# Output projections of two feed-forward blocks: nine pairs of weight tiles by seven products instead of eight, and no plain tile between the two passes

## The chip, the cores and the metric

One core of one Trainium2 chip. The metric is the device time of one execution in microseconds, as the median of several runs. TensorE is called PE in the profile, its weight loads PEld, VectorE DVE, ScalarE ACT, GpSimd POOL, and SyncE, which only issues transfers here, SP.

## The reference

One encoder layer on 512 tokens of width 1024 in float32: a feed-forward block (FFN), a mixer, and a second FFN.

```
def swiglu(x, w_in, w_out):
    gate, up = jnp.split(x @ w_in, 2, axis=-1)
    return (jax.nn.silu(gate) * up) @ w_out        # 1024 -> 2 x 2816 -> 1024

h = swiglu(rmsnorm(x, norm_ffn1_pre[l]), w_ffn1_in[l], w_ffn1_out[l])
x = x + FFN_RESIDUAL_SCALE * rmsnorm(h, norm_ffn1_post[l])
h = mixer(rmsnorm(x, norm_mix_pre[l]), ...)        # gated convolution, two-way mLSTM, output projection
x = x + rmsnorm(h, norm_mix_post[l])
h = swiglu(rmsnorm(x, norm_ffn2_pre[l]), w_ffn2_in[l], w_ffn2_out[l])
x = x + FFN_RESIDUAL_SCALE * rmsnorm(h, norm_ffn2_post[l])
```

The change lies in the output projection of each FFN, `(...) @ w_out`, a sum over 2816 hidden channels, and in three small places around.

## The kernel before

**Precision.** Every operand of a matmul is split into a high part (a rounding copy on ACT, `whi`) and a low part (the rest, a subtraction on DVE, `wlo`), by `split` (L352, L355) or `split_free` (L359, L360). A product is three matmuls: high by high, high by low, low by high. `split` is pinned: its DVE operation keeps its place in program order. `split_free` is not.

**Hidden channels.** 2816 channels are 22 tiles of 128, called k. For each k, `ffn` forms gate and up from 8 k tiles of the input and writes `h[k]`, 128 x 512 (channels by tokens). From the third k on, gate and up together take seven products in place of eight block products (Strassen's scheme in Winograd's form; L498, 20 passes of a loop with the variable `j`).

**Output projection.** The result is four blocks of 128 tokens by two halves of 512 columns: eight banks of PSUM, `acc[tb][half]`. A plain k tile gives 4 x 2 x 3 matmuls of 512 columns (`mm_out`, L673). A pair of k tiles, with the tokens cut in an early and a later half, is a 2 x 2 by 2 x 2 block product and is done by seven products of 2 x 3 matmuls each (`product_out`, L651). The seven sums do not fit in the banks together, so there are two passes over the pairs:

- pass a: products 1, 6, 7, 5 of every pair. Its left factors are sums of quarters of `h` (`left_a`, two pairs at a time, made in place in `h`), its right factors sums of quarters of `w_out` (`w_out_a`). An `a` item of weights is two half tiles and an own quarter (SP) and a quarter added by an accumulating transfer (POOL, L168).
- after the last pair of pass a, `taken` moves the banks into SBUF: a copy on ACT (L661) and six DVE operations (L605), pinned.
- pass b: products 2, 3, 4 of every pair, with `left_b` and `w_out_b`. A `b` item is one tile (SP, L200) and a quarter that POOL adds onto a kept sum (L188).

`SPLIT = (8, 5)` says: eight pairs (16 of 22 tiles) by seven products, and five plain tiles at the end (the tail), token block by token block, each block followed by its norm (`post_norm`). The one tile that is left is done plainly between the passes, and the first `left_b` is formed there.

**Order.** `w_get(n)` hands out the next weights and splits n items ahead. Raw weights go through four buffers (`rawp`), split ones through twelve (`wpool`), and the large tiles `h`, factors, sums through thirteen (`big`). The order on each engine is laid out beforehand by a planner which takes the instruction of the earliest place in the program that is ready by its own reckoning, except where instructions are pinned, or put behind another one by `tc.issue_after`. TensorE's matmuls are not pinned in the output projections.

**Residual.** `x_t` are four tiles of 128 x 1024 in `xpool`, which has just four. In the first FFN they hold x from the start to the end; after it they go to DRAM (`x_d`, L825) and are loaded again late in the mixer (L1322), for the second FFN.

**Mixer.** Behind four projections of one tile each (`plain_o`) comes `weigh_q` (L1101, L1107): four matmuls that spread decay factors, and eight DVE operations that weight the queries by them. `combine_x` forms the sums and splits of the mixer's input for its seven-product groups.

Of the kernel before, what the change touches and what calls it, by code (L numbers as in the profile page):

```python
# [28 lines left out]
SPLIT = ((8, 5), (8, 5))  # L29
# [3 lines left out]
PLAIN = 2  # L33
BW = 528
# [4 lines left out]
def encoder_kernel(ctx: ExitStack, tc: tile.TileContext, a: dict, out: bass.AP):  # L39
# [322 lines left out]
    def rstd(parts, n, mul, tag="rs"):  # L362
        w = parts[0].shape[1]
        acc = None
        for p_ in parts:
            t = sm([P, 4], tag=tag)
            if acc is None:
                pin(nc.vector.tensor_scalar(
                    out=t[:, 0:w], in0=p_, scalar1=mul / n, scalar2=mul * EPS, op0=ALU.mult, op1=ALU.add))
            else:  # L370
                pin(nc.vector.scalar_tensor_tensor(
                    out=t[:, 0:w], in0=p_, scalar=mul / n, in1=acc, op0=ALU.mult, op1=ALU.add))
# [94 lines left out]
    def post_norm(tb, acc, g, mul, after=None, order=(0, 1)):  # L467
        t = [t2() for _ in range(2)]

        def weigh(i):  # L470
            nc.vector.tensor_tensor(out=t[i], in0=acc[i], in1=g[:, blk(i, 512)], op=ALU.mult)

        s0 = sumsq(acc[order[0]])
        weigh(order[0])
        r = rstd([s0, sumsq(acc[order[1]])], D, mul)
        weigh(order[1])
        for i in range(2):
            h = blk(i, 512)
            nc.vector.scalar_tensor_tensor(out=x_t[tb][:, h], in0=t[i], scalar=r, in1=x_t[tb][:, h], op0=ALU.mult, op1=ALU.add)
            if after:  # L480
                after(tb, h)
# [20 lines left out]
    def ffn(xq, between, finish, mid=None, within=None, ahead=(2, 2, 1, 1), late=None, prep=None, block=0):  # L502
# [89 lines left out]
        later, early = slice(256, 512), slice(0, 256)  # L592
# [7 lines left out]

        def hcol(k):
            return h[k // 4][:, k % 4, 0:512]

        def tt(o, a_, b_, op, order=lambda v: None):
            order(nc.vector.tensor_tensor(out=o, in0=a_, in1=b_, op=op))  # L605

        def halves(g):
            if g == 1:
                t = bigt(F32R).rearrange("p q f -> p (q f)")
                return t[:, 0:1024].rearrange("p (g f) -> p g f", g=1), t[:, 1024:2048].rearrange("p (g f) -> p g f", g=1)  # L610
            return tuple(
                bigt(F32R).rearrange("p q f -> p (q f)")[:, 0:2048].rearrange("p (g f) -> p g f", g=2) for _ in range(2))

        def parts(hi, lo, g, at):
            return [{n: (hi[:, i, c:c + 256], lo[:, i, c:c + 256]) for n, c in at.items()} for i in range(g)]

        def group(i):
            g = min(2, seven - i)
            v = h[i // 2].rearrange("p (g e) f -> p g e f", e=2)[:, 0:g, :, 0:512]
            return g, v[:, :, 0], v[:, :, 1]  # L620

        def left_a(i):
            g, a_, b_ = group(i)
            hi, lo = halves(g)
            s1 = t4()[:, 0:256 * g].rearrange("p (g f) -> p g f", g=g)
            tt(s1, a_[:, :, early], b_[:, :, early], ALU.subtract)
            split_free(hi[:, :, 0:256], lo[:, :, 0:256], a_[:, :, later])
            tt(a_[:, :, early], a_[:, :, later], a_[:, :, early], ALU.subtract)
            tt(a_[:, :, later], a_[:, :, early], b_[:, :, early], ALU.add)
            split_free(hi[:, :, 256:512], lo[:, :, 256:512], s1)  # L630
            split_free(hi[:, :, 512:1024], lo[:, :, 512:1024], a_)
            return parts(hi, lo, g, {1: 0, 5: 256, 7: 512, 6: 768})

        def left_b(i):
            g, a_, b_ = group(i)
            hi, lo = halves(g)
            split_free(hi[:, :, 0:512], lo[:, :, 0:512], b_)
            tt(a_[:, :, early], b_[:, :, later], a_[:, :, later], ALU.subtract)
            split_free(hi[:, :, 512:768], lo[:, :, 512:768], a_[:, :, early])
            return parts(hi, lo, g, {4: 0, 2: 256, 3: 512})  # L640
# [48 lines left out]
        hs, plain_n = None, 0  # L689
        ks = {}  # L690
        for at, (kind, n) in enumerate(order):
# [13 lines left out]
            elif kind == "a":  # L705
                if n % 2 == 0 and n:
                    lefts = left_a(n)
                left, right = lefts[n % 2], w_get(1)
                for m in ((1, 6, 7, 5) if n else (6, 7, 5)):
                    product_out(m, left, right, n == 0, n == seven - 1)  # L710
                    if n == seven - 1:
                        taken(m)
            else:
                if n % 2 == 0:
# [3 lines left out]
                for m in (2, 3, 4):  # L718
                    product_out(m, left, right, False, False)

# [449 lines left out]
    weigh_k()  # L1170
    plain_o(3)
    weigh_q()
# [154 lines left out]
    for tb in range(NT):  # L1327
# [12 lines left out]
        xs[tb] = pre_norm(tb, g_pre3)  # L1340

# [36 lines left out]
```

## Time and profile before

| | |
|---|---|
| median of 3 runs | 894.24 us (893.87 to 894.26) |
| the profiled execution | 893.36 us, of which the span is 891.6 us |
| PE, DVE, ACT, POOL busy | 883.4, 716.3, 485.5, 86.6 us |
| granted TensorE clock | 0.999 |
| read from HBM, written | 109.66 MB, 4.19 MB |

The span runs from the first to the last instruction of the program on the core. Busy shares are averages over stages with different limits, so the stages are looked at one by one. A row such as `DVE L355 TENSOR_TENSOR wlo<-raw,whi 128x1024 ... x1` names engine, line, operation, what is written from what, the shape and the count; in front stand start and length in microseconds, behind, in brackets, how long the engine was idle before and what ended that.

### The profile page before, as it was taken

The numbers are of one execution on the slowest core, as the hardware profiler recorded it, in microseconds if no ns is written. First come the engines' busy times: TensorE is split into PE (matmuls) and PEld (weight loads), VectorE is DVE, ScalarE is ACT, GpSimd is POOL, SyncE is SP. The second block draws the span as 40 slices with busy tenths as digits, with TensorE's granted clock in tenths as the row PEclk, the third lists the DMA queues.
The fourth block names the chain that finished last, engine by engine and source line by source line (L and its number), as shares of the span: only waits on it lengthen the run. The fifth ranks groups of instructions, "written<-read, shape, count | busy, mean of one in ns | idle before, by whom it ended". The sixth has DMA issues, their size and how long they took to land.

```text
span 891.6 us, 15212 instructions
## 1 busy us (share of the span) xinstructions
PE 883.4 (99%) x6007; PEld 810.1 (91%) x6007; DVE 716.3 (80%) x1109; ACT 485.5 (54%) x824; POOL 86.6 (10%) x108
## 2 busy tenths in 40 slices
PE   9999999999999999999999999999999999999997
PEld 7999999999988889988888888999999999988885
DVE  5989888888888977688667756898888898797955
ACT  6656455445547645567655535654554555556721
POOL 5000000001140303100111000000000000222000
PEclk9999999999999999999999999999999999999999
DMA  8544434334896651433322621333334324898512
GB/s 238 138 122 118 119 95 115 99 96 122 197 237 181 197 180 73 118 96 105 85 95 89 210 80 56 112 104 109 96 107 127 99 72 142 190 209 220 170 42 93
DMA packets 137234, 114.84 MB, mean 129 GB/s; under 512 B 5173, under 2 KB 115785, under 8 KB 137162
## 3 DMA queue, kind: packets, MB, share of 16 engines
q1 hardware_dynamic: 129354, 97.09, 36.2%
q0 software_dynamic: 7808, 16.78, 9.2%
q8 instruction: 47, 0.77, 0.3%
q14 instruction: 25, 0.20, 0.1%
HBM read 109.66 MB, written 4.19 MB: 128 GB/s over the span
## 4 chain that ended last, share of the span: by engine, by line
PE 98%; DVE 1%; ACT 1%; issue 0%; DVEq 0%; POOLq 0%; POOL 0%; ACTq 0%
PE ps L498 47%; PE ps L651 17%; PE ps L489 10%; PE ps L673 7%; PE ps L1335 5%; PE ps L524 4%; PE ps L859 3%; PE ps L1237 1%; PE ps L407 1%; PE ps L345 1%; PE ps L1245 1%; DVE qt L1107 0%; PE ps L348 0%; PE ps L458 0%; ACT big L352 0%; DVE big L355 0%
## 5 line engine op out<-in xcount | busy, mean ns | idle before, releaser
L498 PE MATMUL ps<-big,whi 128*128 128x256 f32 x2016 | 277.7, 280 | 0.0
L498 PEld LDWEIGHTS ps<-big,whi 128*128 128x128 f32 x2016 | 255.1, 188 | 0.8 <-issue 0.2
L355 DVE TENSOR_TENSOR wlo<-raw,whi 128x1024 fp32r<-128x1024 f32 x165 | 199.9, 1218 | 20.0 <-ACT whi L352 14.0
L352 ACT CAST whi<-raw 128x1024 fp32r<-128x1024 f32 x169 | 174.2, 1050 | 76.0 <-DVE raw L214 30.9
L498 PE MATMUL ps<-big,wlo 128*128 128x256 f32 x1008 | 158.8, 280 | 0.0
L498 PEld LDWEIGHTS ps<-big,wlo 128*128 128x128 f32 x1008 | 136.0, 188 | 0.0
L651 PE MATMUL ps<-whi,big 128*128 128x512 f32 x384 | 119.9, 389 | 0.0
L651 PEld LDWEIGHTS ps<-whi,big 128*128 128x128 f32 x384 | 71.9, 188 | 14.8
L651 PE MATMUL ps<-wlo,big 128*128 128x512 f32 x192 | 74.2, 390 | 0.0
L498 PE MATMUL ps<-big,ws 128*128 128x256 f32 x504 | 68.4, 280 | 0.0
L498 PEld LDWEIGHTS ps<-big,ws 128*128 128x128 f32 x504 | 63.2, 188 | 0.0
L489 PE MATMUL ps<-big,whi 128*128 128x512 f32 x256 | 62.6, 397 | 0.0
L168 POOL DMA_DIRECT2D raw<-in_w_ffn_out_dram x16 | 19.6, 1232 | 435.9 <-DMA raw<-in_w_ffn_out_dram 407.9
L673 PE MATMUL ps<-whi,big 128*128 128x512 f32 x192 | 60.7, 393 | 0.0
L489 PEld LDWEIGHTS ps<-big,whi 128*128 128x128 f32 x256 | 47.6, 188 | 11.1
L576 ACT COPY t<-ps 128x256 f32<-128x256 f32 x40 | 14.9, 372 | 67.1 <-PE ps L498 67.1
L355 DVE TENSOR_TENSOR wlo<-t,whi 128x1024 fp32r<-128x1024 f32 (+1 forms) x42 | 44.7, 1067 | 5.2 <-ACT whi L352 4.8
L352 ACT CAST whi<-t 128x1024 fp32r<-128x1024 f32 (+1 forms) x42 | 38.0, 926 | 18.3 <-DVE t L214 9.7
L673 PEld LDWEIGHTS ps<-whi,big 128*128 128x128 f32 x192 | 36.0, 188 | 8.0
L651 PEld LDWEIGHTS ps<-wlo,big 128*128 128x128 f32 x192 | 36.0, 188 | 7.8 <-DVE wlo L355 0.3
L359 ACT CAST big<-big 128x512 fp32r<-128x512 f32 (+1 forms) x32 | 26.3, 835 | 20.9 <-DVE big L605 10.1
L673 PE MATMUL ps<-wlo,big 128*128 128x512 f32 x96 | 37.6, 392 | 0.0
(233 smaller groups left out, 1323.7 us busy)
## 6 DMA issues: line engine op xcount, KB each, us to landing
raw<-in_w_ffn_in_dram SPq DMA_DIRECT2D x68, 512.0 KB, 4.8
raw<-in_w_ffn_out_dram SPq DMA_DIRECT2D x28, 512.0 KB, 5.2
raw<-in_w_mix_in_dram SPq DMA_DIRECT2D x24, 512.0 KB, 4.0
t<-in_w_ffn_in_dram SPq DMA_DIRECT2D x20, 512.0 KB, 4.6
raw<-in_w_ffn_out_dram SPq DMA_DIRECT2D x32, 256.0 KB, 2.9
raw<-in_w_ffn_out_dram POOLq DMA_DIRECT2D x16, 512.0 KB, 6.9
raw<-in_w_mix_out_dram SPq DMA_DIRECT2D x8, 512.0 KB, 3.5
big<-in_w_ffn_out_dram SPq DMA_DIRECT2D x12, 256.0 KB, 5.5
```

The source lines that it names most:

```text
L168: nc.gpsimd.dma_start(sums.rearrange("p (g f) -> p g f", g=2), top[:, 512:1024].rearrange("p (g f) -> p g f", g=1).broadcast_to([P, 2, 512 ...
L352: latest["hi"] = nc.scalar.copy(out=hi, in_=src)
L355: latest["lo"] = eng.tensor_tensor(out=lo, in0=src, in1=f32(hi), op=ALU.subtract)
L359: nc.scalar.copy(out=hi, in_=src)
L489: nc.tensor.matmul(o, w[ww][:, k, :], xq_tile(xq, (k // 4, xx))[:, k % 4, FULL], start=n == 0, stop=n == 3 * KD - 1)
L498: pin(nc.tensor.matmul(o, ww[:, k, :], x[xx][:, k, :], start=first and n == 0, stop=n == 11, skip_group_check=True))
L524: pin(nc.tensor.matmul(o, ww[:, k, :], xq_hl(xq, (k // 4, th))[xx][:, k % 4, :], start=n == 0, stop=n == 3 * KD - 1))
L576: nc.scalar.copy(a_[:, h1], x[:, h0])
L651: nc.tensor.matmul(acc[tb + t][half], left[n][x][:, blk(t)], right[n][y], start=first and x == y == 0, stop=last_ and x == 1, skip_group_c ...
L673: nc.tensor.matmul(acc[tb][half], hT[hh][:, blk(tb)], w[ww][:, blk(half, 512)], start=fresh and hh == ww == 0, stop=k == NF - 1 and hh == ...
L859: nc.tensor.matmul(pv_[i][:, 0:at.stop - at.start], xv(xx, k, tb), ww[:, k % 2, at], start=n == 0, stop=n == 3 * KD - 1)
L1335: nc.tensor.matmul(acc[half], yy[yi][:, k % 4, blk(tb)], wmo[k][wi][:, blk(half, 512)], start=(n == 0 and yi == 0 and wi == 0), stop=(n == ...
```

## The change

- `SPLIT` becomes (9, 4): nine pairs by seven products, four plain tiles at the end, and none between the passes.
- Left factors can be made into given tiles (`homes`). Those of pass a's third and fourth pair are made in four steps within the gate/up loop (`j` of 11, 13, 15, 17), those of pass b's first two pairs after the seventh pair of pass a. Their homes are the four tiles of `xpool`.
- So the residual is not on the chip in that time: in the first FFN it is read again from the input, in the second from `x_d`, to which the mixer's end now writes it. The four loads stand on POOL's queue behind the second pair of pass b.
- The other left factors of pass a are put behind the weight splits of two pairs before (`marks`, `LAG`).
- `weigh_q` comes before the last `plain_o` instead of behind it.
- In the last block's `post_norm`, the weighing of the second half is put behind the small operation that leads to the norm.

```diff
-SPLIT = ((8, 5), (8, 5))
+SPLIT = ((9, 4), (9, 4))
+LAG = 2
+TURN = 6
+SOON = (11, 13, 15, 17)
...
+    x_src = ([a["x"][0, blk(tb), :] for tb in range(NT)], x_d)
...
-        weigh(order[1])
+        if tb == NT - 1 and after:
+            with tc.issue_after(latest["rs"].ins):
+                weigh(order[1])
+        else:
+            weigh(order[1])
...
+        def left_a(i, home=None):
+            g, a_, b_ = group(i)
...
+                def put(c, v):
+                    for e in range(g):
+                        split_free(hi_[e][:, c:c + v.shape[2]], lo_[e][:, c:c + v.shape[2]], v[:, e])
+
+            def step1():
+                s1 = t4()[:, 0:256 * g].rearrange("p (g f) -> p g f", g=g)
+                tt(s1, a_[:, :, early], b_[:, :, early], ALU.subtract)
+                put(256, s1)
+
+            def step2():
+                put(0, a_[:, :, later])
+                tt(a_[:, :, early], a_[:, :, later], a_[:, :, early], ALU.subtract)
+
+            def step3():
+                tt(a_[:, :, later], a_[:, :, early], b_[:, :, early], ALU.add)
+                put(768, a_[:, :, later])
+
+            def step4():
+                put(512, a_[:, :, early])
...
-        pending = None
+        pending, soon = None, {}
         for j in range(PLAIN, NF):
+            if j == SOON[0]:
+                homes = [xpool.tile([P, D], F32R, tag="x", name=nm("xl")) for _ in range(4)]
+                steps, soon[2] = left_a(2, (homes[0:2], homes[2:4]))
+            if j in SOON:
+                steps.pop(0)()
...
             elif kind == "a":
+                marks.append(latest["lo"].ins)
                 if n % 2 == 0 and n:
-                    lefts = left_a(n)
+                    if n in soon:
+                        lefts = soon[n]
+                    else:
+                        with tc.issue_after(marks[n - LAG]):
+                            lefts = left_a(n)
...
+                if n == TURN:
+                    homes = [xpool.tile([P, D], F32R, tag="x", name=nm("xl")) for _ in range(4)]
+                    with tc.issue_after(marks[n]):
+                        soon["b"] = left_b(0, (homes[0:2], homes[2:4]))
             else:
-                if n % 2 == 0:
+                if n == 0:
+                    lefts = soon["b"]
+                elif n % 2 == 0:
                     with tc.issue_after(mark["taken"].ins):
                         lefts = left_b(n)
...
+                if n == 1:
+                    for tb in range(NT):
+                        x_t[tb] = xtile()
+                        nc.gpsimd.dma_start(x_t[tb], x_src[block][tb])
...
     weigh_k()
+    weigh_q()
     plain_o(3)
-    weigh_q()
...
         xs[tb] = pre_norm(tb, g_pre3)
+        nc.gpsimd.dma_start(x_d[tb], x_t[tb])
```

More of the change, by code (lines that the diff above doesn't have):

```diff
@@ L370, in rstd @@
             else:
-                pin(nc.vector.scalar_tensor_tensor(
-                    out=t[:, 0:w], in0=p_, scalar=mul / n, in1=acc, op0=ALU.mult, op1=ALU.add))
+                latest["rs"] = nc.vector.scalar_tensor_tensor(
+                    out=t[:, 0:w], in0=p_, scalar=mul / n, in1=acc, op0=ALU.mult, op1=ALU.add)
+                pin(latest["rs"])
             acc = t[:, 0:w]
@@ L555, in last, with hcol, tt, halves @@
             nc.vector.tensor_tensor(out=hj[:, h0], in0=x[:, h0], in1=c[:, h0], op=ALU.mult)
-        pending = None
-        for j in range(PLAIN, NF):
+        later, early = slice(256, 512), slice(0, 256)
+        def hcol(k):
+            return h[k // 4][:, k % 4, 0:512]
+        def tt(o, a_, b_, op, order=lambda v: None):
+            order(nc.vector.tensor_tensor(out=o, in0=a_, in1=b_, op=op))
+        def halves(g):
+            if g == 1:
+                t = bigt(F32R).rearrange("p q f -> p (q f)")
+                return t[:, 0:1024].rearrange("p (g f) -> p g f", g=1), t[:, 1024:2048].rearrange("p (g f) -> p g f", g=1)
+            return tuple(
+                bigt(F32R).rearrange("p q f -> p (q f)")[:, 0:2048].rearrange("p (g f) -> p g f", g=2) for _ in range(2))
@@ new lines, in each, with parts, group, put @@
+        def each(v, g):
+            return [v[:, i] for i in range(g)]
+        def parts(hi, lo, g, at):
+            return [{n: (hi[i][:, c:c + 256], lo[i][:, c:c + 256]) for n, c in at.items()} for i in range(g)]
+        def group(i):
+            g = min(2, seven - i)
+            v = h[i // 2].rearrange("p (g e) f -> p g e f", e=2)[:, 0:g, :, 0:512]
+            return g, v[:, :, 0], v[:, :, 1]
+        def left_a(i, home=None):
+            g, a_, b_ = group(i)
+            if home is None:
+                hi, lo = halves(g)
+                def put(c, v):
+                    split_free(hi[:, :, c:c + v.shape[2]], lo[:, :, c:c + v.shape[2]], v)
+                hi_, lo_ = each(hi, g), each(lo, g)
+            else:
+                hi_, lo_ = home
+                def put(c, v):
+                    for e in range(g):
[12 more added lines that the diff above has]
+                put(512, a_[:, :, early])
+            out_ = parts(hi_, lo_, g, {1: 0, 5: 256, 7: 512, 6: 768})
+            if home is not None:
+                return [step1, step2, step3, step4], out_
+            s1 = t4()[:, 0:256 * g].rearrange("p (g f) -> p g f", g=g)
+            tt(s1, a_[:, :, early], b_[:, :, early], ALU.subtract)
+            put(0, a_[:, :, later])
+            tt(a_[:, :, early], a_[:, :, later], a_[:, :, early], ALU.subtract)
+            tt(a_[:, :, later], a_[:, :, early], b_[:, :, early], ALU.add)
+            put(256, s1)
+            put(512, a_)
+            return out_
@@ new lines, in left_b, with put @@
+        def left_b(i, home=None):
+            g, a_, b_ = group(i)
+            if home is None:
+                hi, lo = halves(g)
+                def put(c, v):
+                    split_free(hi[:, :, c:c + v.shape[2]], lo[:, :, c:c + v.shape[2]], v)
+                hi_, lo_ = each(hi, g), each(lo, g)
+            else:
+                hi_, lo_ = home
+                def put(c, v):
+                    for e in range(g):
+                        split_free(hi_[e][:, c:c + v.shape[2]], lo_[e][:, c:c + v.shape[2]], v[:, e])
+            put(0, b_)
+            tt(a_[:, :, early], b_[:, :, later], a_[:, :, later], ALU.subtract)
+            put(512, a_[:, :, early])
+            return parts(hi_, lo_, g, {4: 0, 2: 256, 3: 512})
@@ L591, in ffn @@
         bank = {1: (2, 0), 5: (2, 1), 7: (0, 0), 6: (0, 1), 2: (2, 0), 3: (2, 1), 4: (0, 0)}
-        later, early = slice(256, 512), slice(0, 256)
         ea, eb, xb = bigt(), bigt(), bigt()
@@ L599, in ffn @@
         }
[L601 to L640, printed above, removed]
         begun = {(t, 0) for t in (2, 3)} | {(t, 1) for t in (2, 3)}
@@ L689, in ffn @@
         hs, plain_n = None, 0
+        marks = []
         ks = {}
@@ L705, in ffn @@
             elif kind == "a":
+                marks.append(latest["lo"].ins)
                 if n % 2 == 0 and n:
-                    lefts = left_a(n)
+                    if n in soon:
+                        lefts = soon[n]
+                    else:
+                        with tc.issue_after(marks[n - LAG]):
+                            lefts = left_a(n)
                 left, right = lefts[n % 2], w_get(1)
```

## The prediction

> **What bounds the kernel now.** I read the page's busy times and its chain first, then what TensorE waited for, then the chain piece by piece around the two output projections, then busy time by stretch, and last single instructions where the change puts its hands. Page and waits of PE (engine, line, releaser: us in total, times, longest):
>
> ```profile
> span 891.6 us, 15212 instructions
> PE 883.4 (99%) x6007; PEld 810.1 (91%) x6007; DVE 716.3 (80%) x1109; ACT 485.5 (54%) x824; POOL 86.6 (10%) x108
> PE 98%; DVE 1%; ACT 1%; issue 0%; DVEq 0%; POOLq 0%; POOL 0%; ACTq 0%
> PE ps L345 <- POOL rawg L337: 1.3, 1, 1.3
> PE ps L1186 <- DVE qt L1107: 0.5, 1, 0.5
> ```
>
> TensorE runs from 1.3 to 885.6 us with hardly a hole, and is 98% of the chain. So a matmul taken away is worth its place in the row, provided that the right factors, the left factors and the banks still come in time. The chain in order of time (start, length, what):
>
> ```profile
> 238.91 40.84 PE ps L651 x180
> 279.75 5.49 PE ps L673 x24
> 285.24 32.70 PE ps L651 x144
> 819.77 5.49 PE ps L673 x24
> ```
>
> L651 is a product of a pair, L673 a plain tile. 40.84/180 is 0.227 us from matmul to matmul, 5.49/24 is 0.229. The plain tile between the passes is the row at 279.75 (and at 819.77). Busy time in the stretches pass a, plain tile, pass b (first FFN), pass a and plain tile (second), with the gate/up loop on top (clock, DMA share and GB/s at the end):
>
> ```profile
> 38.50:234.70 196.20, 196.20 (x1670) 196.20 (x1669) 169.37 (x265) 102.98 (x163) 5.06 (x4) 1.00 0.43 119
> 234.70:279.75 45.05, 45.05 (x206) 37.49 (x205) 37.43 (x53) 27.18 (x39) 12.08 (x12) 1.00 0.94 225
> 279.75:285.24 5.49, 5.49 (x25) 4.51 (x25) 5.49 (x8) 3.07 (x4) 0.00 (x0) 1.00 0.40 157
> 285.24:317.93 32.69, 32.69 (x145) 27.00 (x145) 28.00 (x34) 21.26 (x28) 8.64 (x8) 1.00 0.55 175
> 773.10:819.80 46.70, 46.70 (x218) 38.83 (x217) 38.52 (x56) 28.89 (x41) 12.10 (x12) 1.00 0.98 238
> 819.80:825.30 5.50, 5.50 (x25) 4.51 (x24) 5.50 (x9) 2.76 (x5) 0.00 (x0) 1.00 0.15 54
> ```
>
> The third busy figure is DVE. Two things threaten TensorE here: the DMA engines are full through pass a (0.94 and 0.98), and DVE is busy in all of the plain tile (5.49 of 5.49).
>
> **Part by part.** *Matmuls.* A plain k tile is 4 token blocks x 2 halves x 3 = 24 matmuls of 512 columns, a pair done plainly 48; by seven products it is 7 x 2 x 3 = 42. One more pair in each FFN takes away 6 matmuls there, 12 in all: 12 x 0.227 = 2.72 us off the chain. The granted clock is 1.00 in all these rows, so the rate holds. The Trainium skill, "TensorE: Matmul & The Clock Gate", section "Wait — 56ns, not 53.3ns?", gives 215.7 ns from start to start for 512 columns; by it the saving would be 2.59 us. The trace's 0.227 decides.
>
> *The ninth pair's right factors.* Each a item is 1.25 MB (512 KB of halves and 256 KB own on SP, 512 KB accumulated from POOL). The rows of the last item of the first FFN, and of the load behind it, which is the plain tile's; then the same in the second:
>
> ```profile
> 255.16 0.33 SPq L166 DMA_DIRECT2D raw<-in_w_ffn_out_dram  x1
> 258.87 0.33 SPq L202 DMA_DIRECT2D raw<-in_w_ffn_out_dram  x1
> 264.24 1.20 POOL L168 DMA_DIRECT2D raw<-in_w_ffn_out_dram  x1 [1.69 <-DMA raw<-in_w_ffn_out_dram]
> 272.47 0.69 DVE L256 TENSOR_TENSOR t<-big,raw 128x512 f32<-128x512 f32 x1 [1.04 <-DMA raw<-in_w_ffn_out_dram]
> 274.11 0.69 DVE L355 TENSOR_TENSOR wlo<-t,whi 128x512 fp32r<-128x512 f32 x1 [0.95 <-ACT whi L352]
> 274.72 2.36 DVE L355 TENSOR_TENSOR wlo<-raw,whi 128x1024 fp32r<-128x1024 f32 x2
> 794.86 0.33 SPq L166 DMA_DIRECT2D raw<-in_w_ffn_out_dram  x1
> 801.76 0.33 SPq L202 DMA_DIRECT2D raw<-in_w_ffn_out_dram  x1
> 810.01 0.68 DVE L256 TENSOR_TENSOR t<-big,raw 128x512 f32<-128x512 f32 x1
> ```
>
> From first load to sum it is 272.47 - 255.16 = 17.3 us, and 2.3 us more to the low half (274.80). The ninth item takes the raw buffer that the plain tile had, so its loads start at 258.9: sum at 276.2, low half at 278.5. TensorE wants it seven matmuls into the ninth pair, at 279.75 + 7 x 0.227 = 281.3: 2.8 us to spare. Second FFN: 801.76 + 15.15 + 2.3 = 819.2 against 819.77 + 1.59 = 821.4, 2.1 to spare. Against it stands 1.0 MB more (1.25 and the b item's 0.25 accumulated, less the plain 0.5), at 225 GB/s 4.4 us of full DMA. Most of that lands behind the ninth item. I take 0; ends 0 and (4.4 - 2.8) + (4.4 - 2.1) = 3.9 us.
>
> *Left factors ahead.* The third and fourth pairs' a factors move into the gate/up loop: three DVE operations of 512 columns (0.69) and eight splits of 256 (0.42, below), 5.4 us of DVE and eight ACT copies, in four steps of about 1.4. The loop leaves DVE 196.2 - 169.4 = 26.8 us idle, 1.34 per pass of its 20: a step overruns its own pass by 0.1 and the next pass has none. Nothing. The first b factors (two splits of 512, one operation of 512, two splits of 256: 2.9 us) move into pass a. There DVE loses 4.6 (the old steps: five of 0.69, one of 1.22) and the plain tile's 1.2, and gains 3.3 for the ninth item, 2.8 for its left factors, and these 2.9: 37.4 becomes 40.6, in 45.05 + 5.44 = 50.5 us, 80% where it was 83%. If that cover were gone, each microsecond would be a late right factor.
>
> *The turn.* Here the plain tile gave cover: TensorE had 5.49 us in which neither the left factors nor the next right factors were due, and the banks were emptied.
>
> ```profile
> 278.96 3.08 DVE L605 TENSOR_TENSOR big<-ps,big 128x512 f32<-128x512 f32 x5 [0.68 <-ACT big L661]
> 284.83 2.49 DVE L605 TENSOR_TENSOR big<-big 128x512 f32<-128x512 f32 x4
> 287.84 1.22 DVE L355 TENSOR_TENSOR wlo<-raw,whi 128x1024 fp32r<-128x1024 f32 x1
> 818.59 3.08 DVE L605 TENSOR_TENSOR big<-ps,big 128x512 f32<-128x512 f32 x5 [0.29 <-ACT big L661]
> ```
>
> The emptying ends at 282.04, 2.29 us after the turn. Now product 2 follows at once (ACT has copied its banks before: the 0.68 us that DVE waited ended with that copy) for 6 x 0.227 = 1.36 us, then product 3 wants at 281.11 what the fifth of the six operations frees at 281.4: 0.3 us. In the second FFN it frees at 821.06 and is wanted at 821.13. Behind these operations, on a pinned DVE order, stand the splits of the second b item, wanted at turn + 18 x 0.227 + 0.2 = 4.3 us; after the emptying (2.3) its 1.22 is done at 3.5, but at 6.0 if the four left operations (2.49) go first. What stood there besides (plain tile, first b item, first left factors) goes ahead of the turn or away. So 0.3 to 2.0 in the first, 0 to 1.7 in the second, and no gain, as TensorE waits for nothing there now; I take 0.3 each, near the lower ends, since the program names the splits before the left operations: +0.6.
>
> *The query weights swap.* TensorE's one wait inside:
>
> ```profile
> 413.02 1.21 DVE L355 TENSOR_TENSOR big<-t,big 128x1024 fp32r<-128x1024 f32 x1
> 418.70 1.21 DVE L355 TENSOR_TENSOR wlo<-raw,whi 128x1024 fp32r<-128x1024 f32 x1
> 420.05 5.66 DVE L1107 TENSOR_TENSOR qt<-ps,x 64x512 f32<-64x512 f32 x8
> 424.43 1.54 PE L1186 MATMUL ps<-big,big 128*64 128x129 f32 x24 [0.49 <-DVE qt L1107]
> 425.90 1.00 PEld L498 LDWEIGHTS ps<-big,whi 128*128 128x128 f32 x8 [0.17 <-issue]
> ```
>
> The eight operations can start 24 matmuls (5.5 us) sooner; the wait of 0.49 for their banks goes. Late next would be the splits from 413.02 to 419.91, pushed back by 5.66 to 425.6, beside a need at 425.4: at worst 0.2 is given back. I take -0.5; ends -0.5 and +0.2.
>
> *Residual off chip, and the end.* Loads of x and the order at the last block:
>
> ```profile
> x<-xd POOLq DMA_DIRECT2D x4, 512.0 KB, 3.8
> 329.10 1.41 DVE L479 SCALAR_TENSOR_TENSOR x<-t,rs,x 128x512 f32<-128x512 f32 x2
> 886.38 0.16 DVE L371 SCALAR_TENSOR_TENSOR rs<-ss,rs 128x1 f32<-128x1 f32 x1 [2.22 <-ACT junk L382]
> 886.46 0.69 DVE L471 TENSOR_TENSOR t<-ps,gb 128x512 f32<-128x512 f32 x1
> 887.27 1.41 DVE L479 SCALAR_TENSOR_TENSOR x<-t,rs,x 128x512 f32<-128x512 f32 x2
> 228.39 0.42 DVE L584 TENSOR_TENSOR big<-t,t 128x256 f32<-128x256 f32 x1
> ```
>
> The four loads wait on POOL until the second b product frees the buffers, some 8.2 us into pass b (293); even one after the other they are there by 293 + 4 x 3.8 = 308, wanted at 329. Behind them on POOL stand only the V gates' copies. SP's weight loads meet them at a DMA share of 0.55. Nothing; if they met the full engines of pass a, 2 MB at 225 GB/s is 9 us. The four stores after the mixer lie on POOL between the norms' small operations; no wait of PE above ends with one of these. At the end the small DVE operation already runs ahead of the weighing (886.38, 886.46), so fixing that order changes nothing. The tail loses a plain tile per block, already counted.
>
> **Sum.** -2.72 + 0.6 - 0.5 = -2.6. The profiled execution took 893.36 us (891.6 of span, 1.8 around it), 0.9 under the median of the runs, 894.24. So 890.8 for such an execution and 891.6 for the median. A measurement tells about 0.2% (1.8 us) from no change: the gain is not far over it.
>
> **Rivals.** (1) *The ninth item is late.* For: DMA 0.94 and 0.98, DVE's 1.04 us wait for the last item. Against: its loads start no later than the plain tile's did, and the spare times above. Wait 3.9 us at most: 894.24 - 2.6 + 3.9 = 895.5; with half of it 893.6, no change. The Trainium skill, "DMA: Bandwidth & Descriptors", section "Queues, rings and completion order", says that each DMA engine takes turns between the queue rows that have work; by it POOL's accumulations slow SP's loads of the ninth item, which is this rival, and the rows agree in so far as a full DMA made 17.3 us of a load and its sum.
>
> (2) *DVE is behind at the turn* (ends slower). Splits of the first b item, emptying and splits of the second stand pinned in one row. If DVE comes to it as late as it came to the end of the plain tile, TensorE waits 5.49 less product 2's 1.36, 4.1 us in each FFN: -3.2 + 8.3 = +5.1, 899.3. With 3 us each, 897.0. It decides for slower from 2.5 us each on. For: DVE busy in the whole plain tile. Against: a good half of what it did there is gone or goes ahead.
>
> (3) *The swap gives nothing and the turn costs its upper ends*: -2.72 + 3.7 = +1.0, 895.2, no change.
>
> **How the numbers follow.** Forecast 0.60, with its own range 890.7 (nothing lost, -3.2, and 0.3 for the runs) to 892.4; rivals (1) and (3) together 0.22; (2) 0.18. Faster 0.60, same 0.22, slower 0.18. The range goes from 890.4, a little under the sum with all gains, to 896.6, which takes in (1) and (3) and the near part of (2) and leaves about 0.15 outside.
>
> **What would show it.** Right: L651 matmuls 756 instead of 672, and 12 fewer in all with the plain ones; PE's waits still under a microsecond in each output projection; L1186's wait gone; DVE's emptying ending within 2.3 us of the turn. Wrong: a PE wait in pass a's last pair for a low half whose sum waited for DMA (rival 1), or at the turn for DVE, of some microseconds (rival 2), or a row of PE holes in the gate/up loop at the four steps.

## The result, and the profile after

The changed kernel took 889.56 us (median of 6 runs, 887.63 to 889.69) against 893.89 us (6 runs, 892.91 to 894.26) of the kernel before on the same chip: 0.9948 of the time, 95% interval 0.9935 to 0.9962. That is faster by 4.3 us. The forecast was 891.6, 2.6 faster, with a range of 890.4 to 896.6: the sign is right, and the time lies 0.8 us below the range (890.4 less 889.56).

Line numbers have moved: L508 is the old L498, L715 the old L651, L737 the old L673, L725 the old L661, L573 the old L605, L357 and L360 the old L352 and L355, L364 and L365 the old L359 and L360, L169, L171 and L259 the old L166, L168 and L256, L499 the old L489, L1187 the old L1107, L1266 the old L1186, L1415 the old L1335. Kernels with further edits are a few lines off.

The page of the changed kernel, and what PE waited for (us in total, times, longest):

```profile
span 885.9 us, 15298 instructions
PE 877.2 (99%) x5995; PEld 805.8 (91%) x5995; DVE 726.9 (82%) x1145; ACT 492.1 (56%) x850; POOL 93.2 (11%) x124
PE ps L350 <- POOL rawg L342: 1.3, 1, 1.3
PE ps L413 <- DVE t L456: 0.8, 1, 0.8
```

There are 12 matmuls fewer (6007 to 5995), the wait for the weighted queries is gone, and no wait has come in either output projection. The 0.8 us lies in the start (L413 is a transpose in the first norm). The chain, in order of time:

```profile
236.94 83.00 PE ps L715 x366
319.94 17.09 PE ps L737 x74
410.74 0.93 PE ps L1181 x4
419.00 2.79 PE ps L1266 x48
778.58 78.92 PE ps L715 x348
857.50 22.09 PE ps L737 x96
```

Both output projections are now one unbroken run of pair products: 78.92/348 is 0.2268 us for each. The plain tiles behind them cost 22.09/96 = 0.2301. The 48 matmuls of L1266 run in one row of 2.79 us; before, the chain went through the eight DVE operations there, and 24 of the 48 came behind them.

Pass a, pass b, and the second FFN's pass a by stretch (PE, PEld, DVE, ACT, POOL busy; clock, DMA share, GB/s):

```profile
232.70:283.18 50.48, 50.48 (x230) 41.98 (x229) 44.66 (x66) 30.98 (x47) 14.09 (x14) 1.00 1.02 250
283.18:319.94 36.76, 36.76 (x164) 30.45 (x163) 32.48 (x40) 22.69 (x30) 6.67 (x12) 1.00 0.75 240
768.90:820.90 52.00, 52.00 (x242) 43.44 (x242) 44.03 (x67) 32.35 (x48) 14.80 (x15) 1.00 1.04 245
```

The DMA engines are full through pass a (0.94 and 0.98 before, 1.02 and 1.04 now), the residual's loads fill pass b of the first FFN (0.55 before, 0.75 now), and PE is busy in the whole of each stretch all the same. DVE is at 88% in pass a of the first FFN (44.66 of 50.48), not at the 80% of the forecast.

Which stage gave how much is read from the starts of PE's matmuls, from the first of one stage to the first of the next, in one profiled execution each (us). The fourth column holds the mixer from the transposes of its keys to its first seven-product group, with the swap; the rest of the mixer and the plain gate/up tiles of the second FFN are left out:

| kernel | start, norm, plain gate/up | gate/up loop | output projection 1 | transposes of the mixer's keys to seven-product groups | mixer output | gate/up loop | output projection 2 | end |
|---|---|---|---|---|---|---|---|---|
| before | 38.35 | 196.23 | 112.60 | 19.49 | 47.09 | 193.47 | 112.61 | 6.08 |
| same_as_before | 38.35 | 196.23 | 113.35 | 19.49 | 47.09 | 193.47 | 112.55 | 6.08 |
| swap_only | 38.40 | 196.34 | 112.88 | 18.78 | 47.09 | 193.47 | 112.55 | 6.08 |
| moves_only | 38.42 | 196.41 | 112.59 | 18.78 | 47.08 | 193.44 | 112.40 | 6.08 |
| pairs_only | 38.07 | 196.23 | 113.99 | 19.49 | 47.09 | 193.47 | 114.52 | 6.35 |
| after | 36.32 | 196.29 | 111.01 | 18.78 | 47.08 | 193.44 | 110.84 | 6.35 |
| same_as_after | 38.36 | 196.29 | 111.01 | 18.79 | 47.08 | 193.44 | 110.84 | 6.36 |

From before to same_as_after: output projections -1.59 and -1.77, swap -0.70, end +0.28, everything else +0.1, in all 3.7 us. Against same_as_before the first output projection gives 0.75 more; where that comes from is told with the turn, below. The first profile of the changed kernel shows 2.0 us more, all of it in the start; that is no part of the change, as the next part shows.

### The profile page after: what moved, and what is told of

Its sections match the earlier page's. It is cut to its first block, busy times and chain, and to the rows that moved or that the text cites. A ratio compares the mean times of both kernels' runs of the same rounds, so it can differ in the third digit from the quotient of the medians.

```text
span 885.9 us, 15298 instructions
## 1 busy us (share of the span) xinstructions
PE 877.2 (99%) x5995; PEld 805.8 (91%) x5995; DVE 726.9 (82%) x1145; ACT 492.1 (56%) x850; POOL 93.2 (11%) x124
## 4 chain that ended last, share of the span: by engine, by line
PE 96%; DMA 1%; DVE 1%; ACT 0%; POOL 0%; issue 0%; SPq 0%; DVEq 0%; POOLq 0%; ACTq 0%
PE ps L508 47%; PE ps L715 19%; PE ps L499 10%; PE ps L1415 5%; PE ps L737 5%; PE ps L534 4%; PE ps L939 3%; PE ps L1317 1%; DMA raw<-in_w_ffn_in_dram 1%; PE ps L413 1%; PE ps L1325 1%; DMA x<-in_x_dram 0%; PE ps L464 0%; PE ps L1266 0%; POOL wlo L360 0%; PE ps L1293 0%
## 5 line engine op out<-in xcount | busy, mean ns | idle before, releaser
L508 PE MATMUL ps<-big,whi 128*128 128x256 f32 x2016 | 277.0, 280 | 0.0
L508 PEld LDWEIGHTS ps<-big,whi 128*128 128x128 f32 x2016 | 254.9, 188 | 0.8 <-issue 0.2
L357 ACT CAST whi<-raw 128x1024 fp32r<-128x1024 f32 x169 | 174.9, 1053 | 78.2 <-DVE raw L217 22.7
L360 DVE TENSOR_TENSOR wlo<-raw,whi 128x1024 fp32r<-128x1024 f32 x165 | 200.4, 1220 | 19.0 <-ACT whi L357 14.4
L508 PE MATMUL ps<-big,wlo 128*128 128x256 f32 x1008 | 157.8, 280 | 0.0
L508 PEld LDWEIGHTS ps<-big,wlo 128*128 128x128 f32 x1008 | 135.6, 188 | 0.0
L715 PE MATMUL ps<-whi,big 128*128 128x512 f32 x336 | 105.6, 389 | 0.0
L715 PEld LDWEIGHTS ps<-whi,big 128*128 128x128 f32 x336 | 62.9, 188 | 13.0
L171 POOL DMA_DIRECT2D raw<-in_w_ffn_out_dram x18 | 22.0, 1221 | 448.0 <-DMA raw<-in_w_ffn_out_dram 236.5
L508 PE MATMUL ps<-big,ws 128*128 128x256 f32 x504 | 68.4, 280 | 0.0
L715 PE MATMUL ps<-wlo,big 128*128 128x512 f32 x168 | 64.8, 389 | 0.0
L508 PEld LDWEIGHTS ps<-big,ws 128*128 128x128 f32 x504 | 63.2, 188 | 0.0
L499 PE MATMUL ps<-big,whi 128*128 128x512 f32 x256 | 62.6, 397 | 0.0
L499 PEld LDWEIGHTS ps<-big,whi 128*128 128x128 f32 x256 | 47.6, 188 | 11.0
L360 DVE TENSOR_TENSOR wlo<-t,whi 128x1024 fp32r<-128x1024 f32 (+1 forms) x44 | 46.2, 1050 | 1.5 <-ACT whi L357 0.7
L357 ACT CAST whi<-t 128x1024 fp32r<-128x1024 f32 (+1 forms) x44 | 39.6, 915 | 14.0 <-DVE t L217 10.2
L737 PE MATMUL ps<-whi,big 128*128 128x512 f32 x128 | 40.3, 393 | 0.0
L715 PEld LDWEIGHTS ps<-wlo,big 128*128 128x128 f32 x168 | 31.5, 188 | 6.5
L534 PE MATMUL ps<-big,whi 128*128 128x256 f32 x256 | 33.9, 282 | 0.2 <-DVE big L360 0.2
L684 DVE TENSOR_TENSOR t<-ps,t 128x256 f32<-128x256 f32 x40 | 16.9, 423 | 20.7 <-PE ps L508 20.5
L499 PE MATMUL ps<-big,wlo 128*128 128x512 f32 x128 | 32.5, 395 | 0.0
```

The lines of the kernel that those rows point to most:

```text
L171: nc.gpsimd.dma_start(sums.rearrange("p (g f) -> p g f", g=2), top[:, 512:1024].rearrange("p (g f) -> p g f", g=1).broadcast_to([P, 2, 512 ...
L357: latest["hi"] = nc.scalar.copy(out=hi, in_=src)
L360: latest["lo"] = eng.tensor_tensor(out=lo, in0=src, in1=f32(hi), op=ALU.subtract)
L499: nc.tensor.matmul(o, w[ww][:, k, :], xq_tile(xq, (k // 4, xx))[:, k % 4, FULL], start=n == 0, stop=n == 3 * KD - 1)
L508: pin(nc.tensor.matmul(o, ww[:, k, :], x[xx][:, k, :], start=first and n == 0, stop=n == 11, skip_group_check=True))
L534: pin(nc.tensor.matmul(o, ww[:, k, :], xq_hl(xq, (k // 4, th))[xx][:, k % 4, :], start=n == 0, stop=n == 3 * KD - 1))
```

## The experiments

### Copies of both kernels: what is chance

same_as_before and same_as_after are the two kernels unchanged.

> The kernel before, unchanged, run as a kernel of its own so that each execution's span and its profile can be seen. Theory A (the gain is matmuls and the one wait in the mixer; the start varies from execution to execution): ratio 1.000, and where its four bias matmuls at the start run at another rate than in the first profile (3.78 us for four there, 2.25 in the changed kernel's), the span moves by up to 2 us with nothing else changed. Theory B (the changed kernel really starts earlier): the start is as in the first profile in every execution, and no execution falls under 892.

> The changed kernel again. Theory A: ratio 0.9955 to 0.996 (3.6 to 4.0 us), its usual span 888.0; a span of 885.9 comes only where the four bias matmuls at the start take 2.25 us instead of 3.78. Theory B (the changed kernel starts earlier): a short start in most executions.

Measured: same_as_before 894.04 us (11 runs, 891.33 to 894.46), 0.9994 [0.9984, 1.0004]; same_as_after 889.68 (6 runs, 887.09 to 889.97), 0.9954 [0.9942, 0.9966]. Each kernel has two kinds of execution, 2 us or more apart: before at some 893.8 and, in few runs, 891.4; after at some 889.6, and 887.1 and 887.6 in two of twelve. The first instructions of PE tell them apart. The first row is the changed kernel's first profile, the second same_as_after's:

```profile
4.02 2.25 PE L353 MATMUL ps<-g_row,vrows 1*128 1x512 f32 x4
```

```profile
4.01 3.78 PE L353 MATMUL ps<-g_row,vrows 1*128 1x512 f32 x4
```

The same four matmuls take 2.25 or 3.78 us: the full clock was granted at 4.6 us in the one and at about 12 in the other. So the usual span of the changed kernel is 888.0, not 885.9. Of the 14 traces of this case five have the full clock first at 4.0 to 4.6 us, and in three of these five it fell back to half for 3.4 us (flat_tail from 7.5 to 10.9); the other nine have it at 10.6 to 13.0 us. The Trainium skill, "TensorE: Matmul & The Clock Gate", section "What's actually happening", says that the window by which the clock is granted runs freely, so that the moment of the grant differs from run to run. The traces agree that it differs; why it comes as late as 12 us they don't show.

### The parts one at a time

swap_only is the kernel before with the query weights ahead of the last plain tile; pairs_only is it with nine pairs and nothing else; moves_only is the changed kernel with eight pairs.

```diff
 swap_only:                 pairs_only, from before:       moves_only, from after:
+    weigh_q()              -SPLIT = ((8, 5), (8, 5))      -SPLIT = ((9, 4), (9, 4))
     plain_o(3)             +SPLIT = ((9, 4), (9, 4))      +SPLIT = ((8, 5), (8, 5))
-    weigh_q()
```

> The kernel before with only the query weighing ahead of the last plain projection. Theory A: the wait for the banks goes and the stretch from the transposes of k to the first seven-product group shortens by 0.7 us as it did in the changed kernel: ratio 0.9992. My forecast's term was 0.5, its other end -0.2. Theory C (the moves relieve DVE and that is what shortened this stretch): no change here, ratio 1.000.

Measured: 892.95 us (12 runs), 0.9986 [0.9975, 0.9997]. Its stretch went from 19.49 to 18.78, and PE's wait on L1107 is gone from the list. So the swap is worth 0.7 us: the wait of 0.49, and 0.2 around it that the rows don't name.

> The kernel before with only nine pairs and four plain tiles; left factors, residual, order as they were, so at the turn the first b factors are formed after the banks are emptied. Theory A says 12 matmuls of 0.23 us fewer, less what the turn costs without factors made ahead: -2.7 if the turn is covered all the same, ratio 0.997. Theory D (the moves are what makes the turn free): TensorE waits at the turn for left factors, the emptying (2.3 us late), a copy, a subtraction and a split of them, about 3 to 4 us in each FFN, so +3 to +5 net, ratio 1.003 to 1.006.

Measured: 897.48 us (5 runs, 896.70 to 897.72), 1.0041 [1.0029, 1.0053]: slower than before. The waits of PE, and pass a and b of its first FFN in the chain:

```profile
PE ps L651 <- DVE big L360: 3.9, 4, 1.4
238.62 46.31 PE ps L651 x204
291.89 32.71 PE ps L651 x142
```

Pass a ends at 284.93, and from 291.89 on the products run without a hole; the few between wait for the left factors of pass b, which DVE forms only after it has emptied the banks:

```profile
282.54 3.68 DVE L605 TENSOR_TENSOR big<-ps,big 128x512 f32<-128x512 f32 x6 [0.64 <-PE ps L651]
286.13 1.22 DVE L360 TENSOR_TENSOR big<-big,big 128x1024 fp32r<-128x1024 f32 x1
```

Against the changed kernel its projections are 2.98 and 3.68 us longer. This is rival (2), and it is what the ninth pair costs without the moves.

> The changed kernel with eight pairs and the plain tile between the passes again: all moves and the swap, but not the ninth pair. Theory A: only the swap's 0.7 and the 0.1 to 0.3 of small waits in the projections are left, ratio 0.999. Theory D': the moves by themselves free TensorE elsewhere, ratio 0.997 or less.

Measured: 892.25 us (11 runs, 890.51 to 892.64), 0.9981 [0.9972, 0.9989]. The interval overlaps that of swap_only, so in the time a gain of the moves by themselves isn't shown. In the stages the second output projection is 0.15 to 0.2 shorter than in the three eight-pair runs without the moves (112.40 against 112.55 to 112.61); the first (112.59) varies between those by more (112.60 to 113.35). What it does show: with eight pairs the moves hurt nothing.

### What the factors formed ahead are worth

no_a_ahead forms the third and fourth a factors in pass a, like the others. no_b_ahead forms the first b factors after the turn. In no_b_ahead_x_late, besides, the residual's loads stand behind the last accumulating transfer on POOL's queue.

```diff
 no_a_ahead: the four steps at SOON are left out
-                        with tc.issue_after(marks[n - LAG]):
+                        with tc.issue_after(marks[max(0, n - LAG)]):
 no_b_ahead: the block at TURN is left out
-                if n == 0:
-                    lefts = soon["b"]
-                elif n % 2 == 0:
+                if n % 2 == 0:
 no_b_ahead_x_late: from no_b_ahead
-                    nc.gpsimd.dma_start(kept[0], aps[0][:, 0:512], accum_op=ALU.add)
+                    latest["acc"] = nc.gpsimd.dma_start(kept[0], aps[0][:, 0:512], accum_op=ALU.add)
...
-                if n == 1:
-                    for tb in range(NT):
+                if n == seven - 2:
+                    with tc.issue_after(latest["acc"].ins):
+                        for tb in range(NT):
...
```

> The changed kernel, but the third and fourth pairs' a factors are formed in pass a as before, not in the gate/up loop. By the forecast's count DVE then has 4.6 us more in pass a, 45 of 50 us: 90%. Theory G (DVE has room): ratio to the kernel before as the changed kernel's. Theory H (DVE or the thirteen large tiles become the bound in pass a): right factors come late and TensorE waits 1 to 3 us in each FFN, ratio 0.998 to 1.001.

Measured: 889.55 us (5 runs), 0.9957 [0.9945, 0.9969], the same as the changed kernel. PE has no new wait, although DVE is busy for 47.14 of 50.40 us (94%) in pass a of the first FFN there. The a factors ahead are worth nothing here.

> The changed kernel, but the first b factors are formed at the turn, after the banks are emptied, as in the kernel before. Theory D (they must lie ready where no plain tile stands between the passes): TensorE waits about 2 to 4 us at each turn, ratio to the kernel before 1.000 or more. Theory A': DVE reaches them in time anyway, ratio 0.996.

Measured: 905.91 us (4 runs), 1.0139 [1.0126, 1.0152]: 16 us more than the changed kernel, 6.1 in the first output projection and 10.5 in the second, where the turn by itself (pairs_only) cost 3.0 and 3.7. In the changed kernel the first b factors stand in the residual's tiles; with those free, the loads of x are issued in pass a. POOL's issues in the second FFN, and DVE's sum of the ninth item:

```profile
800.47 1.95 POOL L793 DMA_DIRECT2D x<-xd  x2
807.15 2.02 POOL L793 DMA_DIRECT2D x<-xd  x2
812.33 1.25 POOL L171 DMA_DIRECT2D raw<-in_w_ffn_out_dram  x1 [2.26 <-DMA x<-xd]
828.04 0.69 DVE L259 TENSOR_TENSOR t<-big,raw 128x512 f32<-128x512 f32 x1 [6.44 <-DMA raw<-in_w_ffn_out_dram]
```

The ninth item's accumulating transfer (L171) stands behind the x loads on POOL, and from its issue to the sum it is 15.7 us, where transfers of that group take 7.7 from issue to landing in the changed kernel (the median of 18; the ninth item's of the second FFN takes 7.6). PE's new waits, and three stretches (columns as above):

```profile
PE ps L715 <- ACT whi L357: 4.9, 1, 4.9
PE ps L715 <- DVE big L365: 4.3, 3, 1.6
800.00:824.00 24.00, 24.00 (x108) 19.79 (x107) 18.48 (x27) 10.24 (x17) 9.61 (x12) 1.00 1.09 296
824.00:830.00 6.00, 1.12 (x5) 0.64 (x3) 1.61 (x3) 1.92 (x3) 0.00 (x0) 0.90 0.90 208
830.00:836.00 6.00, 6.00 (x15) 4.40 (x15) 5.61 (x8) 4.92 (x7) 0.85 (x1) 0.53 0.64 148
```

The second wait is that for the b factors, at the turns. The first is that for the late transfer: the DMA share is 1.09, PE stands for 4.9 us, and behind that the granted clock is 0.53: 15 matmuls in 6 us where 26 would fit. One late transfer is paid twice. The Trainium skill, "TensorE: Matmul & The Clock Gate", section "What's actually happening", has the clock halved after an idle window of some 3.4 us; a wait of 4.9 followed by 0.53 agrees.

> As the kernel without first b factors ahead, but the four loads of x are put behind the last accumulating transfer of the weights on POOL's queue. In the run before this one they had moved into pass a, since nothing held their buffers any longer, where the DMA engines were full: the ninth item's accumulation took 15.7 us there to land and TensorE waited 5.0 us for it. Theory I (two costs: x in pass a, and the first b factors at the turn): with x late only the turn's waits are left, 3 to 4 us in each FFN as where nine pairs were done without the moves, ratio to the kernel before 1.002 to 1.005. Theory J (the factors at the turn cost it all): about 905 again.

Measured: 894.48 us (12 runs), 1.0007 [0.9997, 1.0016]. The late transfers are gone (PE's one wait on ACT or DVE in the output projections is that for the b factors, 2.7 us), and the turn by itself is left: output projections of 113.40 and 113.27, 2.4 us longer each than the changed kernel's. So of the 16 us some 5 are the b factors and some 11 the x loads in pass a, 3.7 in the first FFN and 8.1 in the second. The first b factors ahead turn the ninth pair from no gain into a gain.

### What a plain matmul costs, and why

The forecast priced every matmul at 0.227 us, but those of the plain tiles take 0.230. The large tiles that hold the plain tiles' left factors have a gap of 16 columns behind each 512. flat_tail makes them without the gap; flat_mixer_out does that for the left factors of the mixer's output too, and flat_mixer_in for all split inputs of the input projections, the gate/up loop's among them. In the tail and the mixer's output the tile in question is the stationary operand of the matmul (128 x 128 in the rows, loaded by PEld); in most input projections, the gate/up loop's too, it is the moving one (128 x 512 or 128 x 256 in the rows).

```diff
 flat_tail:
-                    hs = bigt(F32R)
+                    hs = bigt(F32R).rearrange("p q f -> p (q f)")[:, 0:2048].rearrange("p (q f) -> p q f", f=512)
 flat_mixer_out, besides (flat makes the same view):
-    ym = (bigt(F32R), bigt(F32R))
-    yc = (bigt(F32R), bigt(F32R))
+    ym = (flat(F32R), flat(F32R))
+    yc = (flat(F32R), flat(F32R))
 flat_mixer_in, besides:
-            xq["q"][key] = bigt(F32R)
+            xq["q"][key] = flat(F32R)
```

> The changed kernel with the plain tiles' left factors laid without the gap of 16 columns between rows of 512 in their tile, as the pairs' left factors lie. It asks why a plain matmul comes every 0.230 us and a product's every 0.227. Theory E (the place of the stationary tile does it): 192 plain matmuls at 0.227, 0.6 us less, ratio to the changed kernel 0.9993. Theory F (the tail's other work, or the moving side, does it): still 0.230, no change.

Measured: 888.58 us (5 runs), 0.9942 [0.9930, 0.9953]. The last tail in the chain of flat_tail:

```profile
857.70 21.77 PE ps L737 x96
```

21.77/96 is 0.2268, the price of a pair product, where the changed kernel's row has 22.09, 0.2301. The output projections are 0.40 and 0.32 shorter. Only the place of the left factors differs, so the place is the cause; the medians alone (888.58 and 889.68, with overlapping intervals) would not show it.

> The changed kernel with the tail's left factors and the mixer's output (both stationary sides) laid without the gap of 16 columns after each 512. The tail's matmuls came every 0.227 us instead of 0.230 in the run with that alone. Theory E (the place of the stationary tile): the mixer's output projection, 192 matmuls every 0.232 to 0.233, falls to 0.227 too, 1.0 us less besides the tail's 0.7: ratio to the kernel before 0.9935. Theory F' (it is something of the tail alone): the mixer's projection stays as it was.

Measured: 887.98 us (6 runs), 0.9941 [0.9926, 0.9956]. The mixer's output went from 47.08 to 46.23; its first row in the chain of the changed kernel, then of flat_mixer_out:

```profile
503.51 22.27 PE ps L1415 x96
```

```profile
502.75 21.79 PE ps L1418 x96
```

> As that, and the split inputs of all input projections (the moving side there) without the gap as well. Theory E' (either side's place counts): the mixer's plain column projections, 384 matmuls every 0.233, fall to 0.227, 2.4 us less, and perhaps the 256-column products too. Theory E (the stationary side alone counts): no more than the run with the mixer's output alone.

Measured: 895.20 us (12 runs), 1.0015 [1.0005, 1.0024]: slower. The matmuls of 512 columns again gained. A row of the mixer's column projections in the chain of flat_mixer_out, then of flat_mixer_in:

```profile
374.28 28.04 PE ps L502 x121
```

```profile
379.12 27.46 PE ps L502 x121
```

28.04/121 is 0.2317, 27.46/121 is 0.2269, and here it is the moving operand that lies elsewhere: either side's place counts (Theory E'). But the matmuls of 256 columns lost. The gate/up loop in the chain of flat_mixer_in, beside the changed kernel's:

```profile
37.05 200.16 PE ps L511 x1668
```

```profile
36.48 196.29 PE ps L508 x1668
```

200.16/1668 is 0.1200 us, 196.29/1668 is 0.1177. The loop takes 3.87 us more, and 3.84 in the second FFN. So in these kernels the gap is right for the moving operand of 256 columns and wrong for 512.

best keeps the flat tiles where products are mostly 512 wide (tail, mixer's output and inputs), leaves the gate/up loop as it was, and gives the four matmuls of L353 128 rows in place of one, to see whether the full clock comes sooner:

```diff
+    nc.vector.memset(g_row, 0.0)
...
-                pin(nc.tensor.matmul(g_pre[i], ones, g_row[0:1, blk(i, 512)], start=True, stop=True))
+                pin(nc.tensor.matmul(g_pre[i], ident[:, 0:1].broadcast_to([P, P]), g_row[:, blk(i, 512)], start=True, stop=True))
...
-            xq["q"][key] = flat(F32R)
+            xq["q"][key] = flat(F32R) if "m" in xq else bigt(F32R)
```

> The changed kernel with three things that the runs point to, each read from its own stretch. (1) No gap in the tail's left factors and the mixer's output: output projections 110.6 and 110.5 us, mixer's output projection 46.2, as measured. (2) No gap in the mixer's split inputs alone, where 512-column matmuls prevail, and the gap kept in the FFN's, where it served the 256-column products: stretch of V 58.8, products of the mixer 18.6 and 81.2, together 1.2 us less, and the gate/up loops at 196.3 and 193.4 as in the changed kernel. (3) The four matmuls at the start that spread the first gain, which use one row of the array, use all 128 (127 rows are zeros): theory K (matmuls with one row keep TensorE's clock down: in most executions the full clock was granted at 12 to 13 us only, in the quick ones at 4 to 5) expects the grant by 8 us in most executions and the gate/up loop's start at 36 to 37 us instead of 38.4; theory L (the grant is a matter of when the execution meets the clock's own rhythm) expects 38.4 in most executions still. Under K some 884.8, under L 886.8.

Measured: 886.58 us (5 runs, 885.39 to 888.35), 0.9922 [0.9908, 0.9935], which lies under the changed kernel's own ratio too (same_as_after, 0.9954 [0.9942, 0.9966]). The start in its one profiled execution, the slowest of the five:

```profile
5.76 3.75 PE L357 MATMUL ps<-g_row,ident 128*128 128x512 f32 x4 [1.67 <-DMA g_row<-in_norm_ffn_pre_dram]
```

Four matmuls of 128 rows take 3.75 us, as four of one row did (3.78): the full clock came at 11.8 us, no sooner, and the load of `g_row`, behind the clearing, cost a wait of 1.67, so that the gate/up loop starts at 39.5 us instead of 38.4. So 128 rows are not enough to bring the grant early; whether they make it early more often one trace can't show. What best gains over flat_mixer_out lies in the mixer: its V and key stretch, input products and groups are 0.56, 0.16 and 0.47 shorter. The two intervals overlap, so the order of these two rests on the stages, not on the times.

## Why the prediction was right and wrong

*Matmuls, the main term: right in count, low in price.* 12 fewer, as said. But "12 x 0.227" prices matmuls of two kinds alike. What goes are 48 plain ones for each pair, what comes are 42 of a pair: by the forecast's own rows 48 x 0.229 - 42 x 0.227 = 1.46 each, 2.9 in all; by 0.2303 and 0.2268, the rates of before's last tail (27.64 us for 120) and of the changed kernel's products, 3.06. The step named both rates and then used one. Measured are -1.59 and -1.77, 3.36. The last 0.3 are small holes between products in the kernel before, most of them in pass a of its second FFN:

```profile
779.86 39.91 PE ps L651 x175
```

39.91/175 is 0.2281, and 175 products at 0.2268 would take 0.2 us less; the changed kernel's row of 348 has no such hole.

*The ninth pair's right factors: right.* Nothing was lost. The rows of the ninth item, in the first FFN of the changed kernel:

```profile
254.72 0.33 SPq L169 DMA_DIRECT2D raw<-in_w_ffn_out_dram  x1
273.32 0.69 DVE L259 TENSOR_TENSOR t<-big,raw 128x512 f32<-128x512 f32 x1
274.71 0.69 DVE L360 TENSOR_TENSOR wlo<-t,whi 128x512 fp32r<-128x512 f32 x1
```

From load to sum it is 18.6 us (forecast 17.3), the low half is there at 275.40 and wanted at the turn (283.05) less 17 matmuls, 279.2: 3.8 us to spare (forecast 2.8). In the second FFN sum at 813.22, low half at 815.29, wanted at 816.8: 1.5 to spare (forecast 2.1). Rival (1) did not come, though by 1.5 us only. That the x loads would hurt in pass a stood in the forecast as 9 us of full DMA in each FFN; no_b_ahead paid 3.7 and 8.1 for it.

*The turn: the step that failed.* The forecast put +0.6 here and "no gain, as TensorE waits for nothing there now". The runs show 0, and a gain of 0.75 against an execution of before such as same_as_before's. The forecast took it that the emptying keeps its place, ending 2.29 us behind the turn (2.46 by the start of the first plain matmul, 279.58, which is the measure used from here on). The rows at the first turn before, then of the changed kernel:

```profile
275.88 0.58 ACT L661 COPY big<-ps 128x512 f32<-128x512 f32 x1
276.36 0.62 ACT L352 CAST big<-big 128x512 fp32r<-128x512 f32 x1
277.83 0.61 ACT L352 CAST big<-big 128x512 fp32r<-128x512 f32 x1
278.35 0.58 ACT L661 COPY big<-ps 128x512 f32<-128x512 f32 x1
279.58 0.39 PE L673 MATMUL ps<-whi,big 128*128 128x512 f32 x1
```

```profile
278.72 0.59 ACT L725 COPY big<-ps 128x512 f32<-128x512 f32 x1 [1.62 <-PE ps L715]
280.15 0.59 ACT L725 COPY big<-ps 128x512 f32<-128x512 f32 x1
280.77 3.17 DVE L573 TENSOR_TENSOR big<-ps,big 128x512 f32<-128x512 f32 x5 [0.16 <-ACT big L725]
283.05 0.39 PE L715 MATMUL ps<-whi,xl 128*128 128x512 f32 x1
283.86 1.22 DVE L360 TENSOR_TENSOR wlo<-raw,whi 128x1024 fp32r<-128x1024 f32 x1
286.13 2.23 DVE L573 TENSOR_TENSOR big<-big 128x512 f32<-128x512 f32 x4
```

The first b product (`xl`) starts at 283.05, and the emptying ends at 283.94, 0.9 behind it. In the row of before that the prediction shows, five of the six operations waited 0.68 us for ACT's second copy. That copy now starts 2.9 us ahead of the turn; before, it was 1.2 (278.35 for 279.58). Of these 1.7 us, 1.0 is what stood between the two copies before and doesn't now, two casts of plain tiles' left factors (L352; one tile is gone, the other's cast comes later). The other 0.6 is that product 1, which the first copy waits for, is through earlier in the last pair: that copy starts 4.3 us ahead of the turn (3.7 before). So the forecast followed on DVE what the missing plain tile frees and forgot ACT, which releases DVE here. In the second FFN the emptying ends 1.7 behind the turn (822.30 for 820.62), near the forecast's 1.9 of before, and without a wait for ACT (0.29 before); the fifth operation is through 0.3 us before product 3 wants its bank: the lower end that stood there, 0.

That ACT sets the place of the emptying, and that it can cost TensorE time, is seen in same_as_before. There DVE's five operations wait 1.29 us for ACT's second copy and end at 282.80, and TensorE has small holes behind them, most of them ending with one of DVE's operations: the plain tile takes 5.82 us instead of 5.49, pass b 33.08 instead of 32.70. This is nearly all of the 0.75 by which its first output projection is longer (113.35 against 112.60; swap_only's, 112.88, lies between). The profile of before that the forecast was made from is an execution without these holes. No run moves ACT's copies alone, so how much of the turn is ACT's part and how much the order of the products is read from the rows only. The splits of the second b item go ahead of the four left operations (283.86, 286.13), as was taken.

*Rival (2)* was right on its mechanism and on its price of 3 us each for a kernel without the moves (897.0 forecast, pairs_only 897.48), and rightly not the forecast: its "against" was that the work goes ahead, and no_b_ahead_x_late shows that this is the first b factors.

*The swap: -0.5 for -0.7.* The direction and the place are right; 0.2 more than the wait itself came off its stretch. Rival (3) fell with it.

*Left factors, residual, order at the end: 0.* Right for the a factors (no_a_ahead) and for the loads, which take 5.4 us each in pass b of the first FFN. The count of DVE's work in pass a was 4 us short (44.66 for 40.6): 1.7 are operations of the emptying that now lie ahead of the turn, and 1.9 the splits of the first b item, which came into pass a and were not counted. TensorE lost nothing by it. The end came out 0.28 us longer in every kernel with four plain tiles, with or without the other changes (6.35 against 6.08); it lies behind the last instruction of DVE, and why is open.

*The sum.* From the profiled execution of before to that of same_as_after the change is worth 3.7 us, against 2.6: +0.6 for the turn, +0.6 for the price of plain matmuls and before's holes, +0.2 for the swap, -0.3 for the end. The medians say 4.3. The profiled execution of before took 893.36, half a microsecond under the median of its six runs, 893.89; same_as_before's took 894.04, has the 0.75 at the turn besides, and from its span to that of same_as_after it is 4.3 as well (892.3 to 888.0). The forecast's best case had the turn at 0 already (890.7); what led below it are the dearer plain matmuls, the swap, and the holes of before.

## What to carry to other kernels

When a piece of work goes, price what goes and what comes each at its own row, and follow on every engine what the missing piece frees, above all on the engine that releases the one you watch. Profile the kernel before twice: here a second execution showed a loss at the turn that the first did not. A ninth pair by itself made this kernel slower, since it took away the cover of the turn; the gain came from forming the first factors of the next pass ahead, in tiles whose owner could wait. Tiles freed earlier let their loads start earlier too: where they share a full queue with what PE wants next, hold them back by an order.

## What was not expected of the hardware

- Where an operand lies sets the pace of matmuls: with a gap of 16 columns behind each 512, a row of 512-column matmuls takes 0.230 to 0.232 us each, without it 0.227. This holds for the stationary operand (tail, mixer's output) and for the moving one (mixer's column projections). With 256 columns, where the moving operand was moved, it is the reverse, 0.1177 with the gap and 0.1200 without. Why isn't known from these runs.
- After a wait of 4.9 us the granted clock was half for 6.8 us (no_b_ahead, 828.8 to 835.6).
- In the start the full clock came first at 4.0 to 4.6 us or at 10.6 to 13.0 us, for the same instructions, worth some 2 us; in the one trace with four matmuls of 128 rows in place of one row it came at 11.8.
